# Compression dealt out into the projections, and prompt scores taken in pairs, in a two-layer decoder step

## The chip, the cores and the metric

The kernel runs on one core of one Trainium2 chip. The metric is the device time of one execution in microseconds. The engines are PE (TensorE matmuls), PEld (TensorE weight loads), DVE (VectorE), ACT (ScalarE), POOL (GpSimd) and SP (SyncE, which issues every DMA here).

## The reference

One inference step of a two-layer decoder for a prompt of 512 tokens and 8 x 8 sampled tokens (576 columns together). Layer 0 mixes with a convolution and stick-breaking attention, layer 1 with native sparse attention; each layer then has cross-attention into a memory and a SwiGLU FFN. The change lies in layer 1's mixer:

```python
def compress_blocks(kv, pe, w1, w2):
    ...
    blk = kv.reshape(B, nb, CMP_BLK, G, d) + pe[None, None, :, None, :]
    hid = jax.nn.gelu(jnp.einsum('bnlgd,ldh->bngh', blk, w1))
    return jnp.einsum('bngh,he->bnge', hid, w2)

def odd_mixer(...):
    u = a @ w_in
    ...
    kc = compress_blocks(ck_all, pe_k, w1_k, w2_k)
    vc = compress_blocks(cv_all, pe_v, w1_v, w2_v)
    ...
    o_cmp = jnp.einsum('bgrtn,bngd->btgrd', p_cmp.astype(vc.dtype), vc)
    o_sel = selected_branch(q, to_blocks(sk_all), to_blocks(sv_all), sel_idx, q_pos)
    o_win = window_branch(q, wk_all, wv_all, q_pos, w_pos)
    o = gates[..., 0:1] * o_cmp + gates[..., 1:2] * o_sel + gates[..., 2:3] * o_win
```

For the prompt the selected and the window branch are both a causal softmax attention over all 512 keys, so each needs scores, a softmax, a scaling by the gate and a product with the values.

## The kernel before

Every large product is `dense` (line 283): blocks of 256 output columns; in a block four PSUM groups (columns 0 to 255 and 256 to 575, for each 128 outputs), each group eight k-steps of three matmuls (L304, L305, L306: high and low halves in fp32r). The weights of the next block are loaded into a ring of three `raw` buffers and split (`wblock`, L262 to L272) while the block runs. `tick`, where given, is called after every second k-step and after each group, 16 times in a block.

The source order is a priority, not the order of issue: a planner that runs when the kernel is built places the instructions of each engine, earlier source first among those that its own model holds ready, and each engine then runs that list strictly in order. The trace shows such placing: the page loads of L1134 for the first three row tiles start at 540 us, 500 us ahead of the code around them, and transposes of one step stand between the matmuls of the next.

`odd_mixer` (layer 1) first projects the compressed branch's keys and values (`dense` into `ckv`, 512 columns), then the queries in four blocks `dq(0)` to `dq(3)` of 256 columns, each followed by `rope`. Around them `compress("k")` and `compress("v")` run, each in two halves of 16 positions (`h16`):

- rows: four tiles `kn` from the ring `KN` (three buffers), each of four page loads of 64 KB on SP (L1134), a DVE copy that reorders it (L1135), four PE transposes (L1139), four copies into `bt` (L139, L141); then nine small DVE copies of the prompt's own rows (L1150, L1151). `bt` is one buffer, `xtp`.
- hidden: four loads of first-layer weights `w1`, 512 KB each, into the `raw` ring (L1155), and 32 fp32 matmuls a half (L1161; each stands as two records in the trace, so 64 a half).
- after the second half the GELU and the load of `w2`, then the second-layer product.

The order in the source is: rows of k's first half, `dq(0)`, hidden of it, rows of the second half, `rows_out` (transposes and writes of `ckv`), `dq(1)`, hidden of it, k's second layer, then the same for v around `dq(2)` and `dq(3)`, v's second layer, and the projections of the other keys and values (`blk`).

The prompt's attention is `main`: 32 units (two head groups, four query blocks `j` of width 128 to 512 keys, two pairs of heads, two branches). In a unit `scores` makes four score tiles `z` in the PSUM ring `ACC` (four buffers): two fp32r matmuls (L1539 with the high, L1540 with the low half of the keys) and a bf16 matmul that adds the causal mask (L1541). Then come a maximum on DVE (L1542) and an exponential with its sum on ACT (L1543). After the fourth tile one reciprocal and one product with the gate make the factors `f` (L1546, L1548), and POOL multiplies the four tiles (L1552). The step `values` of an earlier unit, dealt between the tiles, transposes its four tiles key block by key block (L1563) and multiplies with the values (L1573); its first key block needs all four multiplied tiles. The steps are dealt as s s v0 s v1 s v2 v3 ..., where s is one tile's scores.

Of the kernel before, what the change touches and what calls it, by code (L numbers as in the profile page):

```python
# [94 lines left out]
def hybrid_step(ctx: ExitStack, tc: tile.TileContext, off, a, o):  # L95
# [984 lines left out]
    def odd_mixer(l):  # L1080
# [28 lines left out]
        def ev_to(dst, scale=None):  # L1109
            return lambda m, s0, n, p: ev_r(dst[:, m, s0:s0 + n], p, s0, scale)  # L1110
# [11 lines left out]
        dense(w, A, 0, 8, c0, 512, ev_to(ckv), nxt=(w, 0, 8, 0, 256, load_q, paired))  # L1122

        def compress(x):
            W = 161
            hps = [WK("hid0"), WK("hid1")]
            for h16 in range(2):
                bt = xtp.tile([128, 16 * W], FT, tag="bt", name="bt").rearrange("p (c n) -> p c n", n=W)
                for q4 in range(4):
                    kn = KN("cn")  # L1130
                    for i in range(4):
                        src = a["cache_nsa_cmp_" + x][0, ds(pages[q4 * 4 + i], 1)] \
                            .rearrange("a (n c l) g d -> (a n) c (l g d)", n=2, l=2)
                        nc.sync.dma_start(kn[i * 32:i * 32 + 32, 0:512], src[:, h16 * 16:h16 * 16 + 16])  # L1134
                    nc.vector.tensor_copy(kn[:, 512:1024].rearrange("p (g l d) -> p g l d", g=4, l=2),  # L1135
                                          kn[:, 0:512].rearrange("p (l g d) -> p g l d", l=2, g=4))
                    p = WK()
                    for g in range(4):
                        nc.tensor.transpose(p[:, g * 128:g * 128 + 128], kn[:, 512 + g * 128:640 + g * 128], ident)  # L1139
                    pv = p.rearrange("p (g b c) -> p g b c", g=4, c=16)  # L1140
                    for g in range(4):
                        evac(bt[:, :, q4 * 32:q4 * 32 + 32].rearrange("p c (b g) -> p g b c", g=4)[:, g], pv[:, g])
                cb = h16 * 16
                for g in range(4):
                    gp, gg = g // 2, g % 2
                    srow = ckv[gg * 64:gg * 64 + 64, (0 if x == "k" else 2) + gp, 0:TP] \
                        .rearrange("p (n c l) -> p c n l", n=8, l=2)
                    for l2 in range(2):
                        d_ = bt[l2 * 64:l2 * 64 + 64, :, 128:160].rearrange("p c (n g) -> p c n g", g=4)
                        nc.vector.tensor_copy(d_[:, :, :, g], srow[:, cb:cb + 16, :, l2])  # L1150
                nc.vector.tensor_copy(bt[:, :, 160], vt[:, vo["cmp_pe_" + x] + cb:vo["cmp_pe_" + x] + cb + 16])  # L1151
                yield
                for c4 in range(4):
                    w1 = wp.tile([128, 4, 256], FT, tag="raw", name="w1", bufs=3)
                    nc.sync.dma_start(w1, a["cmp_w1_" + x][0].rearrange("l d h -> (l d) h")  # L1155
                                      [(cb + c4 * 4) * 128:(cb + c4 * 4) * 128 + 512]
                                      .rearrange("(c p) h -> p c h", p=128))
                    for c in range(4):
                        cc = c4 * 4 + c
                        for m in range(2):  # L1160
                            nc.tensor.matmul(hps[m][:, :W], w1[:, c, m * 128:m * 128 + 128], bt[:, cc, :],  # L1161
                                             start=cb + cc == 0, stop=cb + cc == 31)
                if h16 == 0:
                    yield
            hid = ar[:, 0:320].rearrange("p (m n) -> p m n", m=2)
            hb = SML(2, "hb")
            for m in range(2):
                nc.vector.tensor_copy(hb[:, m:m + 1], hps[m][:, 160:161])
                nc.scalar.activation(hid[:, m, :], hps[m][:, 0:160], AF.Gelu_apprx_tanh, bias=hb[:, m:m + 1])
# [3 lines left out]
            yield  # L1173

        Vn = ar[:64, 4096:4608].rearrange("p (r f) -> p r f", r=2)
        cres = {}
        ck_, cv_ = compress("k"), compress("v")

        def dq(i):
            dense(w, A, 0, 8, i * 256, 256, ev_to(qT[:, i * 2:i * 2 + 2], 0.125), load_q, paired,  # L1180
                  nxt=(w, 0, 8, i * 256 + 256, 256, load_q, paired) if i < 3 else blk[0])
            rope(qT[:, i * 2:i * 2 + 2])
# [22 lines left out]

        next(ck_)
        dq(0)
        next(ck_)
        next(ck_)
        pump([rows_out(ckv, ("cmp_k", "cmp_v"))], 9)  # L1210
        dq(1)
        next(ck_)
        hid, w2 = cres["k"]
        p = WK()
        for m in range(2):
            nc.tensor.matmul(p[:64, 0:160], w2[:, m, :], hid[:, m, :], start=m == 0, stop=m == 1)
        kc, ksw, kr = ar[:64, 448:608], ar[:64, 608:768], ar[:64, 768:1088]
        kcs = cp.tile([128, 128], FT, name="kcs")
        nc.sync.dma_start(kr, a["c_ropec"])
        nc.vector.tensor_copy(kc, p[:64, 0:160])  # L1220
        nc.scalar.activation(ksw[0:32], p[32:64, 0:160], AF.Copy)
        nc.scalar.activation(ksw[32:64], p[0:32, 0:160], AF.Copy)
        nc.vector.tensor_mul(kc, kc, kr[:, 0:160])
        nc.vector.tensor_mul(ksw, ksw, kr[:, 160:320])
        for hh in range(2):
            nc.vector.tensor_add(kcs[hh * 64:hh * 64 + 64], kc[:, 0:128], ksw[:, 0:128])
        next(cv_)
        dq(2)
        next(cv_)
        next(cv_)  # L1230
        dq(3)
        next(cv_)
        hid, w2 = cres["v"]
        hx = ar[:, 1088:1344]
        hxv = hx.rearrange("p (m g r x n) -> p m g r x n", m=2, g=2, r=4, x=2)
        for m in range(2):
            for gp in range(2):
                for r in range(4):
                    nc.vector.tensor_copy(hxv[:, m, gp, r], hid[:, m, 128:160]
                                          .rearrange("p (n g x) -> p g x n", g=2, x=2)[:, gp])  # L1240
        p = WK()
        for m in range(2):
            nc.tensor.matmul(p[:, 0:64], hid[:, m, 0:128], w2[:, m, :], start=m == 0, stop=m == 1)
        evac(vcs, p[:, 0:64])
        p = WK()
        for m in range(2):
            nc.tensor.matmul(p[:, 0:64], hx[:, m * 128:m * 128 + 128], w2[:, m, :], start=m == 0, stop=m == 1)
        l2 = xtp.tile([128, 2560], FT, tag="bt", name="l2")
        vcz, pcT = l2[:, 0:1024], l2[:, 1024:1536]
        kcd = l2[:, 2048:2144]  # L1250
        nc.vector.memset(kcd, 0.0)
        kcv = kcd.rearrange("p (g x) -> p g x", g=2)
        for hh in range(2):
            nc.vector.tensor_add(kcv[hh * 64:hh * 64 + 64, :, 16 + hh * 8:24 + hh * 8],
                                 kc[:, 128:160].rearrange("p (n g x) -> p x g n", g=2, x=2)[:, hh],
                                 ksw[:, 128:160].rearrange("p (n g x) -> p x g n", g=2, x=2)[:, hh])
        nc.vector.tensor_tensor(vcz.rearrange("p (h d) -> p h d", d=64),
                                p[:, None, 0:64].to_broadcast([128, 16, 64]),
                                C("hsel", 16)[:, :, None].to_broadcast([128, 16, 64]), op=OP.mult)
# [11 lines left out]
        def cmp_prompt():  # L1271
            zt = WK("cmz")
# [222 lines left out]
        dense(w, A, 0, 8, blk[0][3], 256, ev_to(kk_[:, 0:2]), nxt=blk[1])  # L1495
# [36 lines left out]
        def scores(P, gp, j, rp, br):  # L1532
            n = (j + 1) * 128
            nm, sm, f = SML(4, "nm"), SML(4, "sm"), SML(4, "f")
            for x in range(4):
                gg = x // 2
                q = qd[gp, j, rp, gg][:, x % 2]
                z = ACC()
                nc.tensor.matmul(z[:, :n], q, kd[gp][:, gg, br, :n], start=True, stop=False)  # L1539
                nc.tensor.matmul(z[:, :n], q, kl[gp][:, gg, br, :n], start=False, stop=False)  # L1540
                nc.tensor.matmul(z[:, n - 128:n], identb, causb, start=False, stop=True)  # L1541
                last[0] = nc.vector.tensor_reduce(nm[:, x:x + 1], z[:, :n], axis=AX.X, op=OP.max, negate=True)  # L1542
                last[1] = nc.scalar.activation(P[:, x, :n], z[:, :n], AF.Exp, bias=nm[:, x:x + 1],  # L1543
                                               accum_out=sm[:, x:x + 1])
                if x == 3:
                    nc.vector.reciprocal(f, sm)  # L1546
                    f4 = f.rearrange("p (g r) -> p g r", g=2)
# [212 lines left out]
```

## Time and profile before

| what | us |
|---|---|
| runs: median (lowest to highest, 3 runs) | 2161.29 (2157.91 to 2163.09) |
| the profiled execution's own time | 2158.69 |
| its span from the first to the last instruction | 2156.8 |
| PE busy in the span | 2058.1 (95%) |
| TensorE's mean granted clock | 0.982 |

Times in rows are microseconds from the span's start unless marked ns. A matmul's recorded length includes the time in which it overlaps the next one, so the pace of PE is read from the distances between starts. The granted clock is a share of 2.4 GHz; 0.50 is the lower level, 1.2 GHz. The DMA share is a mean over the core's 16 DMA engines.

### The profile page before, as it was taken

The numbers are of one execution on the slowest core, as the hardware profiler recorded it, in microseconds if no ns is written. First come the engines' busy times: TensorE is split into PE (matmuls) and PEld (weight loads), VectorE is DVE, ScalarE is ACT, GpSimd is POOL, SyncE is SP. The second block draws the span as 40 slices with busy tenths as digits, with TensorE's granted clock in tenths as the row PEclk, the third lists the DMA queues.
The fourth block names the chain that finished last, engine by engine and source line by source line (L and its number), as shares of the span: only waits on it lengthen the run. The fifth ranks groups of instructions, "written<-read, shape, count | busy, mean of one in ns | idle before, by whom it ended". The sixth has DMA issues, their size and how long they took to land. (4 is left out here: it accounts for less than half of the span.)

```text
span 2156.8 us, 38247 instructions
## 1 busy us (share of the span) xinstructions
PE 2058.1 (95%) x15545; PEld 1901.2 (88%) x15545; DVE 1045.1 (48%) x1820; ACT 833.3 (39%) x1737; POOL 805.2 (37%) x752
## 2 busy tenths in 40 slices
PE   8999989999999999999878989999999999999998
PEld 7999846977999999999878967667887999999998
DVE  5479886445432332325344667654644432233333
ACT  6354554334332122224233546654443422132231
POOL 4365573412344142334212435553511344142342
PEclk9999998999999999999999989999999999999999
DMA  7454142256222222223344122311355222223232
GB/s 238 149 171 158 39 152 84 87 164 205 84 79 79 79 80 88 88 67 108 100 140 122 55 74 72 89 30 41 127 168 174 70 85 82 79 64 103 79 111 114
DMA packets 219358, 225.17 MB, mean 104 GB/s; under 512 B 13527, under 2 KB 208152, under 8 KB 219110
## 3 DMA queue, kind: packets, MB, share of 16 engines
q1 hardware_dynamic: 219181, 222.73, 33.3%
q8 instruction: 122, 2.00, 0.4%
q14 instruction: 55, 0.44, 0.1%
HBM read 210.04 MB, written 17.08 MB: 105 GB/s over the span
## 5 line engine op out<-in xcount | busy, mean ns | idle before, releaser
L304 PE MATMUL acc<-aH,wh 128*128 128x320 f32 (+1 forms) x2320 | 698.1, 301 | 0.0
L306 PE MATMUL acc<-aH,wl 128*128 128x320 f32 (+1 forms) x2320 | 692.2, 298 | 0.0
L305 PE MATMUL acc<-aL,wh 128*128 128x320 f32 (+1 forms) x2320 | 691.4, 298 | 0.0
L304 PEld LDWEIGHTS acc<-aH,wh 128*128 128x128 f32 x2320 | 442.5, 191 | 5.8 <-issue 4.5
L306 PEld LDWEIGHTS acc<-aH,wl 128*128 128x128 f32 x2320 | 442.3, 191 | 4.3 <-issue 4.1
L305 PEld LDWEIGHTS acc<-aL,wh 128*128 128x128 f32 x2320 | 442.3, 191 | 2.8 <-issue 2.5
L268 ACT ACTIVATE wh<-raw 128x1024 fp32r<-128x1024 f32 (+2 forms) x270 | 260.8, 987 | 433.8 <-PE acc L305 158.8
L272 POOL TENSOR_TENSOR wl<-raw,wh 128x1024 fp32r<-128x1024 f32 (+2 forms) x100 | 229.0, 2293 | 386.2 <-ACT wh L268 356.8
L270 DVE TENSOR_TENSOR wl<-raw,wh 128x1024 fp32r<-128x1024 f32 (+3 forms) x170 | 242.7, 1437 | 92.1 <-ACT wh L268 90.3
L305 PE MATMUL acc<-fL,wh 128*128 128x320 f32 (+1 forms) x592 | 175.6, 297 | 0.0
L304 PE MATMUL acc<-fH,wh 128*128 128x320 f32 (+1 forms) x592 | 175.6, 297 | 0.0
L306 PE MATMUL acc<-fH,wl 128*128 128x320 f32 (+1 forms) x592 | 175.5, 297 | 0.0
L337 DVE TENSOR_TENSOR h<-acc,h 128x320 f32<-128x320 f32 (+1 forms) x176 | 79.7, 455 | 195.6 <-PE acc L306 178.8
L998 POOL TENSOR_TENSOR sg<-sg,rs 128x256 f32<-128x256 f32 (+1 forms) x88 | 87.7, 999 | 154.2 <-ACT sg L997 153.5
L1005 POOL TENSOR_TENSOR fL<-sg,fH 128x256 fp32r<-128x256 f32 (+1 forms) x88 | 89.0, 1011 | 132.8 <-ACT fH L1004 132.0
L221 POOL TENSOR_TENSOR ssq<-ssq,tmp 128x256 f32<-128x256 f32 (+1 forms) x84 | 81.0, 968 | 146.2 <-ACT tmp L220 145.7
L1552 POOL TENSOR_TENSOR nar<-nar,f 128x512 f32<-128x512 f32 (+3 forms) x128 | 92.4, 752 | 106.6 <-DVE f L1548 93.1
L1003 DVE TENSOR_TENSOR sg<-acc,sg 128x256 f32<-128x256 f32 (+1 forms) x88 | 40.1, 456 | 166.3 <-PE acc L306 156.7
L242 DVE TENSOR_TENSOR sg<-acc,rs 128x256 f32<-128x256 f32 (+1 forms) x88 | 39.8, 456 | 159.2 <-PE acc L306 156.5
L306 PEld LDWEIGHTS acc<-fH,wl 128*128 128x128 f32 x592 | 112.5, 190 | 0.0
L304 PEld LDWEIGHTS acc<-fH,wh 128*128 128x128 f32 x592 | 112.5, 190 | 0.0
L305 PEld LDWEIGHTS acc<-fL,wh 128*128 128x128 f32 x592 | 112.5, 190 | 0.0
(433 smaller groups left out, 3958.7 us busy)
## 6 DMA issues: line engine op xcount, KB each, us to landing
raw<-in_w_ffn_gate_dram SPq DMA_DIRECT2D x40, 512.0 KB
raw<-in_w_ffn_up_dram SPq DMA_DIRECT2D x40, 512.0 KB
ck<-in_cache_mem_k_dram SPq DMA_DIRECT2D x32, 512.0 KB
cv<-in_cache_mem_v_dram SPq DMA_DIRECT2D x32, 512.0 KB
raw<-in_w_ffn_down_dram SPq DMA_DIRECT2D x32, 512.0 KB
raw<-in_w_in_even_dram SPq DMA_DIRECT2D x20, 512.0 KB
raw<-in_w_mem_k_dram SPq DMA_DIRECT2D x16, 512.0 KB
raw<-in_w_mem_v_dram SPq DMA_DIRECT2D x16, 512.0 KB
```

Source lines behind the costliest of these rows:

```text
L221: nc.gpsimd.tensor_add(acc, acc, t)
L268: last[1] = nc.scalar.activation(hi, x, AF.Copy)
L270: nc.vector.tensor_sub(lo, x, hi)
L272: nc.gpsimd.tensor_sub(lo, x, hi)
L304: nc.tensor.matmul(po, WH[:, k, ms], H[:, k, s], start=k == 0, stop=False)
L305: nc.tensor.matmul(po, WH[:, k, ms], L[:, k, s], start=False, stop=False)
L306: nc.tensor.matmul(po, WL[:, k, ms], H[:, k, s], start=False, stop=k == nk - 1)
L337: nc.vector.tensor_add(h[:, m, s0:s0 + n], p, h[:, m, s0:s0 + n])
L998: nc.gpsimd.tensor_mul(t, t, rs[s0])
L1003: nc.vector.tensor_mul(t, p, t)
L1005: nc.gpsimd.tensor_sub(HL[:, b0 + m, s0:s0 + n], t, HH[:, b0 + m, s0:s0 + n])
L1552: nc.gpsimd.tensor_tensor(Py, Py, f[:, y:y + 1].to_broadcast([128, n]), op=OP.mult)
```

## The change

1. The compression is cut into generators that `dense` calls at its ticks: `cmp_rows` (rows; one step loads and reorders a tile, the next transposes it), `cmp_hidden` (hidden; two matmuls a tick), `finish_k`, `finish_v`. Rows of k's first half run in the `ckv` projection, hidden of one half and rows of the next run together in one `dq`, `rows_out` and hidden of v's second half in `dq(3)`, `finish_v` in the first `blk` projection.
2. `bt` has two places, by halves: `xtp` and the start of `S2`, which is free until the `blk` projections write there.
3. `w1` leaves the `raw` ring for the two buffers of `KT`, loaded one ahead.
4. `scores` takes its four tiles in two pairs: both masks first, then the four fp32r matmuls, two maxima, two exponentials; then, as a step of its own, the pair's reciprocal, its product with the gate and its two multiplications on POOL. The number of steps of a unit (four) and the dealing order stay.

The work computed is the same, except that there are 64 reciprocals and 64 gate products of two columns where there were 32 of each of four.

```diff
-        def compress(x):
...
+        def cmp_rows(x, h16):
+            if h16:
+                bt = S2[:, 0:16 * W].rearrange("p (c n) -> p c n", n=W)
+            else:
                 bt = xtp.tile([128, 16 * W], FT, tag="bt", name="bt").rearrange("p (c n) -> p c n", n=W)
...
+                nc.vector.tensor_copy(kn[:, 512:1024].rearrange("p (g l d) -> p g l d", g=4, l=2),
+                                      kn[:, 0:512].rearrange("p (l g d) -> p g l d", l=2, g=4))
+                yield 1
...
+                yield 1
...
+        def w1_load():
+            while w1_todo and len(w1s) < 2:
+                x, c = w1_todo.pop(0)
+                w1 = KT("w1").rearrange("p (c h) -> p c h", c=4)
...
+        def cmp_hidden(x, h16):
...
+                for c in range(4):
+                    cc = c4 * 4 + c
+                    for m in range(2):
+                        nc.tensor.matmul(hps[x][m][:, :W], w1[:, c, m * 128:m * 128 + 128], bt[:, cc, :],
+                                         start=cb + cc == 0, stop=cb + cc == 31)
+                    if c == 3:
+                        w1_load()
+                    yield 1
...
+        dense(w, A, 0, 8, c0, 512, ev_to(ckv), nxt=(w, 0, 8, 0, 256, load_q, paired), tick=run((rows["k", 0], 4, 3)))
+        pump(rows["k", 0], 99)
+        cmp_new("k", 0)
+        w1_load()
...
+        dq(0, ([cmp_hidden("k", 0)], 1, 1), (rows["k", 1], 0, 2))
+        cmp_new("k", 1)
+        dq(1, ([cmp_hidden("k", 1)], 1, 1), (rows["v", 0], 0, 2))
+        cmp_new("v", 0)
+        dq(2, ([cmp_hidden("v", 0)], 1, 1), (rows["v", 1], 0, 2), ([finish_k()], 2, 3))
+        cmp_new("v", 1)
+        dq(3, ([cmp_hidden("v", 1)], 1, 1), ([rows_out(ckv, ("cmp_k", "cmp_v"))], 0, 3))
...
+        dense(w, A, 0, 8, blk[0][3], 256, ev_to(kk_[:, 0:2]), nxt=blk[1], tick=run((fv, 2, 4)))
...
-            for x in range(4):
...
-                    for y in range(4):
-                        Py = P[:, y, :n]
-                        nc.gpsimd.tensor_tensor(Py, Py, f[:, y:y + 1].to_broadcast([128, n]), op=OP.mult)
-                yield 1
+            for gg in range(2):
+                zs = [ACC() for r in range(2)]
+                for z in zs:
+                    nc.tensor.matmul(z[:, n - 128:n], identb, causb, start=True, stop=False, skip_group_check=True)
+                for r, z in enumerate(zs):
+                    q = qd[gp, j, rp, gg][:, r]
+                    nc.tensor.matmul(z[:, :n], q, kd[gp][:, gg, br, :n], start=False, stop=False, skip_group_check=True)
+                    nc.tensor.matmul(z[:, :n], q, kl[gp][:, gg, br, :n], start=False, stop=True, skip_group_check=True)
...
+                yield 1
+                fx = f[:, gg * 2:gg * 2 + 2]
+                nc.vector.reciprocal(fx, sm[:, gg * 2:gg * 2 + 2])
+                nc.vector.tensor_mul(fx, fx, gkv[:, j, gp, rp * 2:rp * 2 + 2, gg, 1 + br])
+                for x in (gg * 2, gg * 2 + 1):
+                    nc.gpsimd.tensor_tensor(P[:, x, :n], P[:, x, :n], f[:, x:x + 1].to_broadcast([128, n]),
+                                            op=OP.mult)
                 yield 1
```

In a `run` job the two numbers are the first tick and the distance in ticks at which the generator advances one step.

## Rows read from the trace of the kernel before

**Rows 1.** The page's head and part 1: span; engine busy us (share) xinstructions

```profile
span 2156.8 us, 38247 instructions
...
PE 2058.1 (95%) x15545; PEld 1901.2 (88%) x15545; DVE 1045.1 (48%) x1820; ACT 833.3 (39%) x1737; POOL 805.2 (37%) x752
```

**Rows 2.** Stretches: us, busy us (xinstructions) by engine, granted clock, DMA share, GB/s

```profile
1022.00:1052.00 30.00, 30.00 (x234) 30.00 (x234) 14.59 (x32) 7.14 (x16) 7.64 (x7) 1.00 0.26 74
...
1052.00:1186.00 134.00, 110.54 (x755) 107.11 (x754) 62.35 (x157) 44.91 (x80) 22.08 (x20) 0.92 0.44 131
...
1246.00:1300.00 54.00, 47.67 (x299) 31.24 (x300) 38.72 (x72) 26.52 (x66) 21.59 (x21) 0.84 0.23 66
...
1300.00:1400.00 100.00, 95.74 (x790) 68.81 (x786) 67.82 (x175) 68.43 (x201) 51.46 (x72) 1.00 0.29 81
...
1400.00:1500.00 100.00, 91.13 (x652) 69.98 (x652) 54.77 (x128) 49.17 (x145) 49.44 (x68) 0.98 0.09 27
```

**Rows 3.** Waits of PE in 1052 to 1186: waiter <- releaser: us, times, longest

```profile
PE wk L1139 <- DVE cn L1135: 10.4, 4, 4.6
...
PE hid L1161 <- DMA w<-in_cmp_w_k_dram: 5.5, 2, 3.9
```

**Rows 4.** DMA view of 1058 to 1071: queue, packets, MB, share; then issues

```profile
q1 hardware_dynamic: 374, 0.66, 13.2%
...
cn<-in_cache_nsa_cmp_k_dram SPq DMA_DIRECT2D x7, 64.0 KB
```

**Rows 5.** Two more stretches, columns as in rows 2

```profile
1086.00:1088.00 2.00, 2.00 (x19) 2.00 (x18) 0.81 (x3) 0.41 (x1) 0.00 (x0) 1.00 1.00 291
...
1107.00:1111.00 4.00, 1.45 (x11) 1.21 (x9) 2.66 (x5) 0.81 (x1) 1.32 (x2) 1.00 0.35 118
```

**Rows 6.** Timeline of SyncE's issues and of PE: start, us, line, xcount [idle <-releaser]

```profile
540.80 10.79 SPq L1134 DMA_DIRECT2D cn<-in_cache_nsa_cmp_k_dram  x12
...
1048.32 3.15 SPq L1134 DMA_DIRECT2D cn<-in_cache_nsa_cmp_k_dram  x4
...
1098.88 5.74 SPq L1134 DMA_DIRECT2D cn<-in_cache_nsa_cmp_v_dram  x7
...
1104.73 0.40 SPq L1155 DMA_DIRECT2D w<-in_cmp_w_k_dram  x1
...
1112.38 1.98 PE L1161 MATMUL hid<-bt,w 128*128 128x161 f32 x6 [3.93 <-DMA w<-in_cmp_w_k_dram]
```

**Rows 7.** Waits of PE in 1240 to 1505, columns as in rows 3

```profile
PE ntp L1563 <- POOL nar L1552: 13.7, 29, 1.5
```

**Rows 8.** Groups by shape, 1240 to 1505: xcount | busy, mean ns | idle

```profile
L1552 POOL TENSOR_TENSOR nar<-nar,f 128x512 f32<-128x512 f32 x32 | 35.5, 1139 | 36.5 <-DVE f L1548 30.5 <-PE wk L1424 5.8
...
L1546 DVE RECIPROCAL f<-sm 128x4 f32<-128x4 f32 x32 | 5.6, 175 | 9.6 <-ACT nar L1543 9.2
```

**Rows 9.** Timeline of POOL and PE around the scores, columns as in rows 6

```profile
1254.94 5.01 POOL L1552 TENSOR_TENSOR nar<-nar,f 128x512 f32<-128x512 f32 x4 [6.90 <-DVE f L1548]
...
1385.12 0.48 PE L1539 MATMUL acc<-kd,qd 128*128 128x512 f32 x1
...
1385.43 0.40 PE L1540 MATMUL acc<-kl,qd 128*128 128x512 f32 x1
...
1385.67 0.23 PE L1541 MATMUL acc<-causb,identb 128*128 128x128 bf16 x1
...
1385.71 0.48 PE L1539 MATMUL acc<-kd,qd 128*128 128x512 f32 x1
```

**Rows 10.** Timeline of PE in the compression, columns as in rows 6

```profile
1069.30 6.74 PE L1161 MATMUL hid<-bt,w 128*128 128x161 f32 x48
...
1080.67 0.36 PE L304 MATMUL acc<-aH,wh 128*128 128x256 f32 x1
...
1080.87 0.28 PE L305 MATMUL acc<-aL,wh 128*128 128x256 f32 x1
...
1080.99 0.28 PE L306 MATMUL acc<-aH,wl 128*128 128x256 f32 x1
```

More of the change, by code (lines that the diff above doesn't have):

```diff
@@ new lines, in cmp_new @@
+        def cmp_new(x, h16):
+            bt, cb = bts[x, h16], h16 * 16
+            for g in range(4):
+                gp, gg = g // 2, g % 2
+                srow = ckv[gg * 64:gg * 64 + 64, (0 if x == "k" else 2) + gp, 0:TP] \
+                    .rearrange("p (n c l) -> p c n l", n=8, l=2)
+                for l2 in range(2):
+                    d_ = bt[l2 * 64:l2 * 64 + 64, :, 128:160].rearrange("p c (n g) -> p c n g", g=4)
+                    nc.vector.tensor_copy(d_[:, :, :, g], srow[:, cb:cb + 16, :, l2])
+            nc.vector.tensor_copy(bt[:, :, 160], vt[:, vo["cmp_pe_" + x] + cb:vo["cmp_pe_" + x] + cb + 16])
@@ L1172, in compress, with run, f, dq @@
             cres[x] = hid, w2
-            yield
+        def run(*jobs):
+            n = [0]
+            def f():
+                for gens, first, every in jobs:
+                    if n[0] >= first and (n[0] - first) % every == 0:
+                        pump(gens, 1)
+                n[0] += 1
+            return f
+        rows = {k: [cmp_rows(*k)] for k in (("k", 0), ("k", 1), ("v", 0), ("v", 1))}
+        dense(w, A, 0, 8, c0, 512, ev_to(ckv), nxt=(w, 0, 8, 0, 256, load_q, paired), tick=run((rows["k", 0], 4, 3)))
+        pump(rows["k", 0], 99)
+        cmp_new("k", 0)
+        w1_load()
         Vn = ar[:64, 4096:4608].rearrange("p (r f) -> p r f", r=2)
-        cres = {}
-        ck_, cv_ = compress("k"), compress("v")
-        def dq(i):
+        def dq(i, *jobs):
             dense(w, A, 0, 8, i * 256, 256, ev_to(qT[:, i * 2:i * 2 + 2], 0.125), load_q, paired,
-                  nxt=(w, 0, 8, i * 256 + 256, 256, load_q, paired) if i < 3 else blk[0])
+                  nxt=(w, 0, 8, i * 256 + 256, 256, load_q, paired) if i < 3 else blk[0], tick=run(*jobs))
+            for gens, _, _ in jobs:
+                pump(gens, 99)
             rope(qT[:, i * 2:i * 2 + 2])
@@ L1204, in rows_out @@
                 yield 1
[L1206 to L1216, printed above, removed]
         kc, ksw, kr = ar[:64, 448:608], ar[:64, 608:768], ar[:64, 768:1088]
         kcs = cp.tile([128, 128], FT, name="kcs")
-        nc.sync.dma_start(kr, a["c_ropec"])
@@ L1220, in odd_mixer @@
[L1220 to L1256, printed above, removed]
@@ L1271, in cmp_prompt @@
         def cmp_prompt():
+            l2 = l2_[0]
+            pcT, kcd = l2[:, 1024:1536], l2[:, 2048:2144]
             zt = WK("cmz")
@@ L1534, in scores @@
             nm, sm, f = SML(4, "nm"), SML(4, "sm"), SML(4, "f")
-            for x in range(4):
[L1536 to L1547, printed above, removed]
-                    nc.vector.tensor_mul(f4, f4, gkv[:, j, gp, rp * 2:rp * 2 + 2, :, 1 + br]
-                                         .rearrange("p r g -> p g r"))
-                    for y in range(4):
-                        Py = P[:, y, :n]
-                        nc.gpsimd.tensor_tensor(Py, Py, f[:, y:y + 1].to_broadcast([128, n]), op=OP.mult)
```

131 lines of the change are left out of this document (84 added, 47 removed).

## The prediction

> **What bounds the kernel now.** I read the page's busy shares first: PE is busy for 2058 of 2157 us, no other engine for half of that [rows 1]. So only what keeps PE idle, or slow, can be won. Then the view of stretches, over the part that the diff touches. In the `ckv` projection PE is busy throughout at a granted clock of 1.00. From there to the end of the compression, 1052 to 1186, it is busy for 110.5 of 134 us at a clock of 0.92: 23.5 us idle, and (1 - 0.92) x 110.5 = 8.8 us of busy time lost to stretches at the lower level, 1.2 GHz; together 32.3 us. In the prompt's attention the three stretches from 1246 to 1500 show 6.3, 4.3 and 8.9 us idle, and clocks of 0.84, 1.00 and 0.98, so 7.6 + 1.9 = 9.5 us lost; together 29.0 us [rows 2]. These 61 us are all that the two halves of the change can recover.
>
> The view of waits names the causes. In the compression PE waits 10.4 us for the reordering copy of a row tile and 5.5 us for k's first-layer weights [rows 3]; in the attention 13.7 us for POOL's multiplications [rows 7]. The DMA view says why rows and weights are late. From 1058 to 1071 page loads run alone, seven of them issued inside that stretch: 0.66 MB in 13 us is 51 GB/s, and the share of 13.2% of 16 engines is 2.1 engines [rows 4]. A load of all engines moves 291 GB/s at a share of 1.00 [rows 5]. So queued page loads do not spread: each occupies one pair of engines for 64 KB / 50 GB/s = 1.3 us, a row tile 5.2 us. The weights that share this pair queue behind: a `w1` issued at 1104.73, after seven page loads, is used at 1112.38, 7.65 us later [rows 6], while PE is busy for 1.45 of 4 us and the DMA engines are 35% busy [rows 5].
>
> The Trainium skill (DMA: Bandwidth & Descriptors, Why a DMA increments its semaphore by 16 and not by 1) says that a copy runs on the largest number of engines up to 16 that divides the slowest dimension of both sides, and on the lowest-numbered ones; a page's slice has a slowest dimension of 2. By that all page loads here share one and the same pair, which the rows suggest but do not show, and no order of the source can spread them; if they did spread, the 11 us of lateness below would be zero and the sum 40.5 instead of 29.5 us.
>
> **The change, compression.** The edits and their costs:
>
> *Filling.* Hidden and transposes go between the dense matmuls, in time to be waited for much later than they are loaded. The three first row tiles are loaded at 540 us already [rows 6] and should be again. With k's first half transposed at ticks 7, 13, 19 and 25 of the `ckv` projection's 32 (some 0.9 us each, from 1022 on), their buffers come free from about 1028 on, not 1048, so the pair of DMA engines starts some 20 us earlier. If nothing else were late, all 32.3 us would come back.
>
> *What the pair of engines still holds.* A tick in `dq` is two dense k-steps and four hidden records. Dense: 96 matmuls at 30.0/234 = 0.128 us [rows 2] = 12.3 us a block; hidden: 64 records at 6.74/48 = 0.14 us [rows 10] = 9.0; 16 transposes at about the same 0.13 = 2.1; switches (below) 1.3; together 24.7 us a block, 6.2 us for a quarter of it. In that quarter the pair has to move one row tile (5.2), its part of one `w1` (512 KB at 291 GB/s, 1.8) and of the next projection weights (256 KB, 0.9): 7.9 us. Where the next rows are loaded at full pace, in `dq(0)` and `dq(1)`, eight quarters, PE can be late by 8 x 1.7 = 13.6 us; `dq(2)` and `dq(3)` have slack. The head start from the `ckv` projection takes a part of it: nothing if the queue is full when `dq(0)` begins, all of it at best. The buffers of k's first half come free one by one up to some 7 us before that, each followed by a load of 5.2, so the queue begins nearly empty; a `w1` behind an empty queue lands within its quarter, and the lead of 6.2 - 1.8 us less its issue and landing, some 2 us, covers the first one or two quarters. The other six and a half cost 1.7 each: 11 us, all of it waits on `w1`; bounds 0 and 13.6.
>
> *Own buffers for `w1`.* With two buffers a load is issued when its predecessor's predecessor is done and needed a quarter (6.2 us) later. In the trace the bad case took 7.65 us; SP adds up to 7 page issues x 0.82 = 5.7 us ahead of it [rows 6], though usually four. That lateness is the 11 us above, not a second one. The projection weights no longer share the ring with `w1`; nothing in the rows charges PE for that, so zero.
>
> *Switches.* After fp32 transposes the first dense matmul starts 0.20 us before the second, against 0.12 for the next [rows 10]: 0.08 us to enter. 64 hidden ticks make 64 entries, 5.1 us, of which blocks of hidden paid perhaps 1 before: 4 us more.
>
> *The clock.* If the 11 us gather in a few stalls of 3 to 4 us, like the longest ones before (3.9 and 4.6 [rows 3]), the lower level follows some of them. I keep 2 us of the 8.8 as lost.
>
> *Moved work.* `rows_out` goes from between `dq(0)` and `dq(1)` to `dq(3)`, with its ten writes on SP; there no page loads are queued, so zero. `finish_k` and `finish_v` go into blocks with PE work beside them; v's two products waited 1 to 2 us before. DVE, busy for 62 of 134 us, and ACT, for 45, get nothing new; if a copy that waits for a page blocked DVE for 3 us, the four `ACC` buffers cover three groups, about 9 us. A `bt` in `S2` and the 64 x 2 small copies cost nothing then.
>
> Sum: 32.3 - 11 - 4 - 2 = 15 us won; from 5 (each of 14 reloads later by 0.7 us than in the walk) to 28.
>
> **The change, scores.** *POOL.* Before, four multiplications follow the fourth exponential: 4 x 1.139 = 4.6 us at 512 keys [rows 8], and the first block in the trace waited 6.9 us for its factors, then took 5.0 [rows 9]. Now two tiles are multiplied while the other two are scored, and the second pair is scored one dealing step earlier. The last tile is ready 2 x 1.139 = 2.3 us sooner at 512 keys. All 29 waits on POOL sum to 13.7 us, none longer than 1.5 [rows 7]; a shift of that size ends most. What is late next is DVE and ACT: the second pair's maxima and exponentials. I take 10, bounds 0 (another wait ends last) and 13.7.
>
> *Order on PE.* A tile starts every 0.59 us: 0.31 from the high to the low half, 0.24 to the mask, 0.04 on [rows 9]. The 0.31 against 0.24 is the entry after the mask; in pairs it is paid once for two tiles: 64 x 0.07 = 4.5, less the second mask of a pair, not covered by a long matmul, about 0.02 each: 3 us, bounds 0 and 4.5.
>
> *Costs.* 32 more reciprocals (0.175 us [rows 8]) and as many gate products of about the same cost put 11 us on DVE, busy for 161 of 254 us [rows 2], and each reciprocal now stands on DVE behind the pair's two exponentials, with evacuations behind it. A pair takes two of four `ACC` buffers at once. I take 3 us on the path, bounds 0 and 8.
>
> *The clock.* The longest slow stretch follows the first unit's waits on POOL. If these go, the clock stays up: half of 9.5, 4.5 us; bounds 0 and 9.5.
>
> The first block's multiplications took 5.01/4 = 1.25 us each, the mean is 1.14 [rows 8, 9]. The Trainium skill (SBUF — State Buffer, SBUF: two separate sides) says that a GpSimd instruction and a VectorE one with two SBUF inputs lock one port pair in turn for a whole instruction, which speaks against multiplying beside more DVE work. If all 32 x 2 multiplications that now start earlier at 512 and 384 keys lost 0.11 us so, that would be 7 us on POOL, and the sum 22.5 instead of 29.5; the rows cannot tell this cause from others.
>
> Sum: 10 + 3 - 3 + 4.5 = 14.5 us won; from 0 to 26.
>
> Both: 29.5 us. PE stands at 95% over the whole span [rows 1], and neither half touches what follows these stages, so a gain is kept to the end. The profiled execution took 2158.7, 2.6 under the median of 2161.3; from the median, 2131.8, from the profiled one 2129.2. I say 2131.
>
> **The rivals.** (1) *The pair of engines decides.* Page loads, not order, set the compression's end: the same bytes, the same pair. It then recovers only the start's part, 5 us, and the scores 12: 2144. For it: constant 51 GB/s; against it: 20 us of earlier start. (2) *The planner does not follow.* The lists are placed by its model; it can bunch hidden again or put the pair's second half where the old fourth tile was. Half of both gains: 2146. (3) *Slower: late weights at every reload.* Two buffers, a quarter of 6.2 us, and queue plus landing of 7.65 + 3.3 (four page issues) make each of 14 reloads late by 4.7 us, 66 us, with the clock down at each, 8 more; less 32 recovered and 14.5 from the scores: 27 longer, 2188. It decides from a mean lateness of (32 + 14.5 - 4)/14 = 3 us. For it: one measured 7.65; against it: that one stood behind seven page loads.
>
> **How the numbers follow.** Forecast 0.63, (1) 0.13, (2) 0.11, (3) 0.13. The forecast's own range is 2107 (gains of 28 and 26) to 2148 (13 in all); (1) and (2) lie a few us to either side of their times. The range is 2107 to 2152; out of it are (3) and the tails. What a measurement can tell from no change is about 0.2%, 4 us. Faster: 0.62 of the forecast, 0.11 of (1), 0.09 of (2), 0.82; the same: 0.06, the rest of these three and of (3); slower: 0.12, from (3).
>
> **What would show it.** Right: in the stretch of the compression PE idle falls from 23.5 to about 11 us, with the waits on `w1` (`KT`) ahead of those on rows, and page loads still at 50 GB/s; hidden stands in groups of four records between dense matmuls; the wait of transposes on POOL falls under 5 us and the clock from 1246 to 1300 rises over 0.9. Wrong: waits on `w1` over 40 us, hidden in runs of 48 as now, or waits of the score tiles on ACT in place of those on POOL.

## The result, and the profile after

The kernel after takes 2128.6 us (median of 4 runs, 2128.2 to 2129.0), the one before 2162.2 beside it: a ratio of 0.9846 (95% interval 0.9828 to 0.9864), 33.6 us less. The forecast was 2131.0, in a range of 2107 to 2152. The time was hit; what stands behind it was hit only in part, because terms that were too low and too high offset each other.

The profiled execution of after took 2129.0 us. Its page's head and part 1, for [rows 1]:

```profile
span 2127.2 us, 38324 instructions
...
PE 2045.2 (96%) x15545; PEld 1902.4 (89%) x15545; DVE 1058.4 (50%) x1884; ACT 834.0 (39%) x1737; POOL 803.1 (38%) x752
```

Three marks of the timeline part the two halves of the change: the first dense matmul of the `ckv` projection, the write of the sampled tokens' gates on SP, after the projections (L1500 before, L1544 after), and the first activation of the next norm, after the attention. In after they stand here (start, us, engine, line):

```profile
1021.87 0.28 PE L304 MATMUL acc<-aH,wh 128*128 128x256 f32 x1
...
1206.13 0.34 SPq L1544 DMA_DIRECT2D gd<-nar  x1
...
1476.76 0.51 ACT L213 ACTIVATE aH<-h,vt 128x256 fp32r<-128x256 f32 x1 [1.52 <-DVE h L337]
```

Before they stand at 1019.90, 1215.15 and 1507.21. So the *compression* (first to second mark) went from 195.25 to 184.26 us, 11.0 less, and the *attention* (second to third) from 292.06 to 270.63, 21.4 less. Together 32.4; the spans differ by 29.6 because after reaches the first mark 2.0 us later and loses 0.8 behind the third. The 2.0 are no effect of the change: in the runs below the first mark lies between 1017.8 and 1022.8, over code that is the same. The lengths between marks repeat better than whole times: kernels with the same code for a stage agree within 1.4 us in the compression and within 2.1 in the attention (table below), and the reading goes by them.

The stretches of after, columns as in [rows 2]; the first two end the compression, the last three are the attention but for its first 31 us:

```profile
1052.00:1158.00 106.00, 91.93 (x633) 89.84 (x631) 52.36 (x114) 38.04 (x69) 19.39 (x17) 0.92 0.43 132
1158.00:1206.13 48.13, 45.76 (x334) 43.76 (x334) 29.73 (x60) 25.78 (x38) 15.64 (x14) 1.00 0.23 71
...
1237.00:1290.00 53.00, 45.31 (x312) 30.60 (x310) 41.53 (x84) 27.98 (x72) 23.62 (x24) 0.94 0.23 67
1290.00:1390.00 100.00, 95.39 (x820) 72.43 (x816) 78.12 (x212) 68.87 (x203) 57.21 (x76) 1.00 0.30 88
1390.00:1476.76 86.76, 86.12 (x658) 70.54 (x657) 52.80 (x149) 47.80 (x140) 43.04 (x64) 1.00 0.16 40
```

Cut into PE's idle time, time lost to the lower clock level ((1 - clock) x busy) and the rest, which is busy time at full clock, each by the same marks:

| stage | idle before, after | lost clock before, after | rest before, after |
|---|---|---|---|
| compression | 24.9, 16.4 | 8.8, 7.4 | 161.5, 160.5 |
| attention | 19.5, 13.0 | 9.6, 2.7 | 262.9, 254.9 |

The compression won 8.5 us of idle time and hardly any clock. The attention won 6.5 us of idle time, 6.9 of clock, and 8.0 in which PE was booked as busy. The split is rough. The clock has two places only; summed over slices of 2 us, after's lost clock is 7.3 us in the compression and 3.3 in the attention (9.5 before). Kernels of the table below that share a stage's code differ too: 4.5 to 7.3 us of lost clock in after's compression (four kernels), in the attention 6.6 to 9.5 with the scores of before (three) and 3.1 to 4.6 with those of after (eight). The rest moves little: in those attentions it is 263.0 to 264.1 us and 254.2 to 254.7.

What PE waited for in after, in the compression (1022 to 1206) and then in the attention (from 1206); columns as in [rows 3] and [rows 7]:

```profile
PE hid L1180 <- DVE hb L1190: 3.9, 1, 3.9
PE hid L1180 <- DMA w<-in_cmp_w_k_dram: 3.7, 2, 3.2
PE hid L1180 <- DVE kvA L141: 3.3, 1, 3.3
PE hid L1180 <- issue: 2.2, 1, 2.2
PE hid L1180 <- DMA w<-in_cmp_w_v_dram: 1.7, 1, 1.7
...
PE ntp L1609 <- POOL nar L1597: 4.8, 6, 1.6
PE wk L1414 <- DVE csz L1410: 2.5, 1, 2.5
```

The copies of rows no longer head the list, and POOL's part fell from 13.7 us to 4.8, as forecast. But weights make only 5.4 us of the compression's waits; 9.4 stand on DVE and on "issue", which the prediction put at nothing. The timeline shows what these are (DVE and PE around 1116, then DVE and ACT ahead of the wait of 3.3 us, which ended at 1088.59):

```profile
1116.59 0.43 DVE L1137 COPY cn<-cn 128x512 f32<-128x512 f32 x1 [3.34 <-DMA cn<-in_cache_nsa_cmp_v_dram]
...
1118.01 0.19 DVE L1190 COPY hb<-hid 128x1 f32<-128x1 f32 x2
...
1118.27 1.42 PE L1180 MATMUL hid<-bt,w 128*128 128x161 f32 x4 [3.90 <-DVE hb L1190]
```

```profile
1080.36 0.43 DVE L1137 COPY cn<-cn 128x512 f32<-128x512 f32 x1 [3.69 <-DMA cn<-in_cache_nsa_cmp_v_dram]
...
1080.93 0.48 DVE L244 SCALAR_TENSOR_TENSOR nq<-acc,rs 128x320 f32<-128x320 f32 x1
...
1081.44 2.80 ACT L1102 ACTIVATE nar<-nq 32x576 f32<-32x576 f32 x4 [4.34 <-DVE nq L244]
```

DVE stands for 3.34 us at the reordering copy of a row tile, which waits for its page. Behind it, in DVE's fixed order, stands the small copy `hb` that frees the PSUM tiles that v's hidden writes; PE waits 3.90 us for that. So the late page is the cause here too, by way of DVE's queue. The 2.2 us at 1055 came in the same way: DVE waited 2.87 us at a copy for its page until 1053.29, then a `bt` copy, then PE. The 3.3 us came by one step more. DVE stood for 3.69 us at a copy for its page until 1080.36; behind it stood the evacuation of a dense group whose last matmul had started at 1076.36. `rope` on ACT and DVE needs that evacuation, and the copies of rows into hidden's input stood behind `rope`. So in the trace all 9.4 us lead back to DVE standing at a copy for its page.

### The profile page after: what moved, and what is told of

Same layout as the page of the kernel before. It is cut to its first block, busy times and chain, and to the rows that moved or that the text cites. A ratio compares the mean times of both kernels' runs of the same rounds, so it can differ in the third digit from the quotient of the medians.

```text
span 2127.2 us, 38324 instructions
## 1 busy us (share of the span) xinstructions
PE 2045.2 (96%) x15545; PEld 1902.4 (89%) x15545; DVE 1058.4 (50%) x1884; ACT 834.0 (39%) x1737; POOL 803.1 (38%) x752
```

## The experiments

Compression and attention are measured between the marks above, in one profiled execution each; times are medians, ratios those to the kernel before on the same chip.

| kernel | us | ratio (95% interval) | compression | attention |
|---|---|---|---|---|
| before | 2162.2 | 1 | 195.25 | 292.06 |
| after | 2128.6 | 0.9846 (0.9828 to 0.9864) | 184.26 | 270.63 |
| compression alone | 2150.1 | 0.9939 (0.9924 to 0.9955) | 184.25 | 291.57 |
| scores alone | 2139.5 | 0.9897 (0.9880 to 0.9913) | 193.87 | 270.11 |
| after, pages spread | 2107.1 | 0.9739 (0.9724 to 0.9753) | 165.38 | 271.86 |
| before, pages spread | 2134.0 | 0.9864 (0.9845 to 0.9883) | 168.75 | 292.54 |
| after, pairs multiplied late | 2142.8 | 0.9914 (0.9895 to 0.9933) | 185.26 | 285.07 |
| after, single tiles multiplied early | 2128.1 | 0.9844 (0.9823 to 0.9864) | 183.99 | 268.77 |
| after, row copy on POOL | 2125.2 | 0.9833 (0.9815 to 0.9851) | 182.42 | 271.39 |
| after, `w1` in the `raw` ring | 2123.0 | 0.9829 (0.9810 to 0.9848) | 181.44 | 271.32 |
| pages spread, again | 2108.3 | 0.9762 (0.9737 to 0.9787) | 165.16 | 271.26 |
| pages spread, `w1` in the `raw` ring | 2105.4 | 0.9748 (0.9726 to 0.9770) | 163.46 | 270.14 |
| pages spread, hidden in bunches of eight | 2105.8 | 0.9746 (0.9724 to 0.9768) | 162.60 | 272.18 |
| pages spread, single tiles multiplied early | 2101.7 | 0.9729 (0.9707 to 0.9752) | 165.30 | 266.84 |

### Each half alone

The edit puts the `scores` of the one kernel into the other; nothing else changes.

> The new compression with the scores of before (tiles one by one, four multiplications at the end). Theory of the traces: between the start of the ckv projection and the gate's write the trace of after is 11.0 us shorter (195.25 to 184.26), and nothing of that comes from the scores, so 2162 - 11 = 2151. By the prediction's sum this half wins 15: 2147. Rival: the two halves need each other (the earlier end of the compression lets the first unit start with its keys ready), then each alone wins less than its part: over 2155.

> The paired scores with the compression of before. Theory of the traces: from the gate's write to the next stage after is 21.4 us shorter (292.06 to 270.63), so 2162 - 21.4 = 2141, with POOL's wait of PE near 5 us and the clock of the first stretch near 0.94. By the prediction's sum 14.5: 2148. Rival: halves depend on each other: under 10 us won, over 2152.

Ratios of 0.9939 and 0.9897 are 13.2 us (9.7 to 16.4) and 22.3 us (18.8 to 26.0) of 2162.8. Their sum, 35.5, is the 33.6 of both within the intervals, and each stage's length is that of after in the kernel that has the new half and about that of before in the other. The halves do not need each other. The lengths read from the traces of after, 2151 and 2141 for the halves, were the better forecast; the prediction's sums, 2147 and 2148, were not.

### Do the page loads share one pair of DMA engines?

```diff
-                        .rearrange("a (n c l) g d -> (a n) c (l g d)", n=2, l=2)
-                    nc.sync.dma_start(kn[i * 32:i * 32 + 32, 0:512], src[:, h16 * 16:h16 * 16 + 16])
+                        .rearrange("a (n c l) g d -> c (a n) (l g d)", n=2, l=2)
+                    nc.sync.dma_start(kn[i * 32:i * 32 + 32, 0:512], src[h16 * 16:h16 * 16 + 16])
...
-                pv = p.rearrange("p (g b c) -> p g b c", g=4, c=16)
+                pv = p.rearrange("p (g b c n) -> p g b c n", g=4, c=16, n=2)
```

The copies into `bt` follow the same order. The bytes, the pieces of 2 KB and the number of loads stay.

> The kernel after, with each page load read in the order (16 positions, 2 blocks) instead of (2, 16): same bytes, same number of loads, slowest dimension 16; the copies behind the transposes put the columns back. If a page load sits on one pair of engines because its slowest dimension is 2, it now goes over 16: page loads run at over 200 GB/s while they are alone, a tile takes about 1 us instead of 5.2, and the waits that stand behind late pages go: 2.2 + 3.7 + 3.9 + 1.7 = 11.5 us idle and about 4 to 5 of the 7.4 us of clock, so 2128.6 - 16 = 2113 (2108 to 2119). Rival (the rate of 50 GB/s is that of a queue of small pieces of 2 KB, whatever the engines): no change in rate and time, 2126 to 2130. Rival (the fixed order of DVE and SP holds the stalls): loads fast, time above 2123.

> The kernel before with the same reading order of page loads. If the one pair of engines made most of the loss of before, the waits on the reordering copy (10.4 us) and on weights (8.0) go with part of 8.8 us of clock: 15 to 22 us won, about 2143, and dealing out would be worth little beside it. If the order (rows and hidden in blocks with no dense work between) made it, then PE still waits in row blocks for the chain copy, transposes, copies: under 8 us won, 2155 or more.

The DMA view of 1047 to 1053, first of after, then of after with pages spread (40 slices of 0.15 us: tenths of the 16 engines' time, and GB/s; then the issues, with the time to landing at the end):

```profile
DMA  9551122212111111111111111111111111111111
GB/s 273 150 99 44 58 96 99 96 68 75 65 41 55 55 55 55 41 55 41 55 55 55 55 41 55 55 41 55 55 55 41 55 55 41 55 55 55 55 41 55
...
cn<-in_cache_nsa_cmp_k_dram SPq DMA_DIRECT2D x6, 64.0 KB
```

```profile
DMA  0059100283004640015400000000000000000000
GB/s 14 14 137 259 41 27 0 68 259 110 0 0 82 205 150 0 0 55 219 164 0 0 0 0 0 0 0 0 0 0 0 0 0 0 0 0 0 0 0 0
...
cn<-in_cache_nsa_cmp_k_dram SPq DMA_DIRECT2D x3, 64.0 KB, 2.2
```

In after a queue of page loads runs at an even 41 to 55 GB/s without end. Spread, each load is a burst of up to 259 GB/s, landed 2.2 us after its issue, and between two bursts there is nothing: now SP's issuing, not the transfer, sets the pace. So the pair was real, and the time follows: 21.5 us between the two medians, 18.9 of them in the compression; at 2107.1 it lies just under the 2108 to 2119 expected. The stretch and the largest wait of after with pages spread:

```profile
1052.00:1158.00 106.00, 102.21 (x770) 100.86 (x769) 61.22 (x143) 45.72 (x80) 23.96 (x21) 1.00 0.48 141
...
PE hid L1180 <- DMA w<-in_cmp_w_v_dram: 1.7, 1, 1.7
```

Idle time between the marks falls from 16.4 to 5.5 us, and the clock is 1.00 throughout: 10.9 + 7.4 us. In the old order the same edit does still more, 26.5 us of the compression; its waits on the copy (10.4 us, [rows 3]) and on weights shrink to these, and the largest that stays is 2.6 us for a copy into `bt`:

```profile
PE wk L1139 <- DVE bt L141: 2.6, 1, 2.6
PE wk L1139 <- DVE cn L1135: 1.1, 1, 1.1
...
PE hid L1161 <- DMA w<-in_cmp_w_k_dram: 0.2, 1, 0.2
PE hid L1161 <- DMA w<-in_cmp_w_v_dram: 0.2, 1, 0.2
```

So dealing out is worth 11.0 us where pages are slow and 3.4 (168.75 less 165.38) where they are not: it covered part of a loss that could be taken away at its source. (The 3.4 are one trace against another, where the stage repeats within 1.4.) The Trainium skill (DMA: Bandwidth & Descriptors, Why a DMA increments its semaphore by 16 and not by 1) lets a copy run on the largest number of engines up to 16 that divides the slowest dimension of both sides; from 2 to 16 in that dimension is what this edit changes, and the bursts agree.

### Who holds the hidden matmuls up: DVE's queue or the pages?

```diff
-                nc.vector.tensor_copy(kn[:, 512:1024].rearrange("p (g l d) -> p g l d", g=4, l=2),
+                nc.gpsimd.tensor_copy(kn[:, 512:1024].rearrange("p (g l d) -> p g l d", g=4, l=2),
```

> The kernel after with the reordering copy of a row tile on POOL instead of DVE. A copy that waits for its page then no longer holds up DVE's later work. If the stalls of 2.2 us (before hidden of k) and 3.9 us (hidden of v on the copy of hb) come from DVE's queue standing behind a copy that waits for a page, they go, with the half-clock time behind them: 6 to 9 us won, 2120 to 2122. If the pages themselves set the end (a transpose needs the copy anyway), the waits move to the transposes: within 2 us, 2127 to 2130. If POOL's splits for dense are now held up instead: slower, over 2131.

```profile
PE hid L1180 <- DMA w<-in_cmp_w_k_dram: 10.1, 4, 5.9
PE hid L1180 <- DMA w<-in_cmp_w_v_dram: 5.3, 2, 3.6
```

The waits on DVE and on issue, 9.4 us in after, are gone, and the waits on weights went from 5.4 to 15.4 us. The compression is only 1.8 us shorter, its idle time 16.8 us for 16.5, the time 2125.2 for 2128.6 with intervals that overlap. That lies between the two cases expected, 6 to 9 us and nothing. DVE's queue was the way that the lateness took, not its size: whatever first needs something that the pair delivers late is charged with the wait.

### Own buffers for the weights

```diff
-                w1 = KT("w1").rearrange("p (c h) -> p c h", c=4)
+                w1 = wp.tile([128, 4, 256], FT, tag="raw", name="w1", bufs=3)
```

> The kernel after with w1 back in the raw ring of three buffers that it shares with the projection weights, all else dealt out as in after. The prediction put the own buffers at zero beside the lateness of the pair of engines: 2128.6, within 3. Rival (own buffers matter: in the ring a w1 waits for the split of the projection weights before it, and the projection weights for hidden): each of 14 loads later by 1 us or more, and the clock down behind them: over 2145.

> Spread page loads and w1 back in the raw ring of three. On the kernel after this moved the compression from 184.3 to 181.4 us. If that was the third buffer giving late weights more room, it is worth nothing once pages no longer hold the weights up: compression within 1 us of 165.4, 2106 to 2108. If own buffers matter (projection weights held up by w1): compression over 168, 2110 or more. If sharing is better by itself: under 163.5.

With slow pages the compression is 2.8 us shorter without own buffers, with spread pages 1.7 (163.46 against 165.16), little over the 1.4 us within which the stage repeats. The whole times point the same way, their intervals overlap. The own buffers are no part of the gain; a small loss is likely and not shown beyond doubt. With slow pages the time, 2123.0, missed the 2128.6 "within 3" that was expected. Why sharing should be better is not tested.

### What a switch between hidden and dense costs

```diff
-                    yield 1
+                    if c % 2:
+                        yield 1
...
-        dq(0, ([cmp_hidden("k", 0)], 1, 1), (rows["k", 1], 0, 2))
+        dq(0, ([cmp_hidden("k", 0)], 1, 2), (rows["k", 1], 0, 2))
```

The other three `dq` likewise.

> The kernel after with spread page loads (as in the third experiment), once more, as the base of the three beside it on the same chip: 2107, compression 165.4 us from the first matmul of the ckv projection to the gate's write.

> Spread page loads and hidden in bunches of eight records at every second tick, so 32 switches from hidden to dense in place of 64. By the prediction's price of 0.08 us a switch: 2.6 us won, compression 162.8. By the cycle read in after (six dense matmuls and four hidden records in 1.25 us, their sum apart 0.72 + 0.56 = 1.28) a switch costs nothing: within 0.7 us of 165.4.

The compression went from 165.16 to 162.60, the 2.6 us that the price of 0.08 gives. But the idle time in it shows another way to that number: the waits listed for PE sum to 4.7 us in the base and to 2.2 with bunches (v's weights' wait of 1.7 is gone). That leaves 0.1 us for 32 switches. The time in which PE is busy between the marks, where a switch would be booked, agrees: 159.9 us in the base and 159.7 with bunches, both at a clock of 1.00. So does the timeline of after (one cycle of PE):

```profile
1061.06 0.71 PE L1180 MATMUL hid<-bt,w 128*128 128x161 f32 x4
1061.50 0.39 PE L304 MATMUL acc<-aH,wh 128*128 128x256 f32 x1
1061.72 0.28 PE L305 MATMUL acc<-aL,wh 128*128 128x256 f32 x1
...
1062.31 0.71 PE L1180 MATMUL hid<-bt,w 128*128 128x161 f32 x4
```

The first dense matmul does stand 0.22 us before the second, 0.10 over the pace of [rows 10]. But the four hidden records ahead of it take 0.44 from their start to its start, not 4 x 0.14 = 0.56. The cycle is 1.25 us, and six dense at 0.12 and four hidden at 0.14 make 1.28.

### Order on PE or early multiplication?

Of the two edits of `scores` each kernel keeps one: pairs with everything multiplied after the second pair, or single tiles with the mask last, of which every second is followed by

```diff
+                if x % 2:
+                    fx = f[:, gg * 2:gg * 2 + 2]
+                    nc.vector.reciprocal(fx, sm[:, gg * 2:gg * 2 + 2])
...
+                    for y in (gg * 2, gg * 2 + 1):
```

> The kernel after, but the pairs keep only their order on PE; one reciprocal, one gate product and all four multiplications stand after the second pair, as before. What is lost against after is the early multiplication alone. By the prediction's terms that is 10 (waits on POOL) + 4.5 (clock) less about 1.5 of the 3 us of costs: 2128.6 + 13 = 2142. If by the traces the order on PE won 7.9 and the rest 13.5 (6.6 idle, 6.9 clock): 2142 as well, with PE's wait for POOL back over 10 us. Rival: the multiplications' start matters little because the values come two units later: under 5 us lost, 2133.

> The kernel after, but tiles are scored one by one with the mask last, as before; each two tiles are multiplied as soon as the second is scored. What is lost is the order on PE (and the second step of a pair is one tile, not none). Prediction's term: 3 (0 to 4.5): 2131.6. By the traces 7.9 us less busy time of PE with the idle time and the clock set apart: 2136.5. Rival: nothing lost, 2128.6, where the busy time fell only because there are fewer restarts after waits.

> Spread page loads, tiles scored one by one with the mask last, each two multiplied as soon as they are scored. On the kernel after this left the time as it was (attention 268.8 us against 270.6). If pairing on PE is worth nothing beside early multiplication: attention 269 to 272, 2105 to 2109. If that was chance and pairing is worth the 4.5 us of its pace: attention over 274, 2111.

Waits of PE on POOL in the attention, first pairs multiplied late, then single tiles multiplied early:

```profile
PE ntp L1611 <- POOL nar L1599: 13.1, 23, 1.3
```

```profile
PE ntp L1606 <- POOL nar L1594: 4.1, 6, 2.2
```

Pairs without the early multiplication keep 13.1 us of waits on POOL and win 7.0 us of 21.4. Single tiles with it win 23.3, all and a little more. So the early multiplication is the gain, and the order on PE, worth 7 us alone, adds nothing to the length beside it. Of those 7 us, 6.4 are clock and 2.3 busy time at full clock (summed over slices of 2 us), less 1.7 of added idle time. The clock differs by up to 2.9 us between kernels with the same scores, so how much of the 6.4 the order makes is open. With spread pages single tiles are even 4.4 us shorter than pairs (266.84 against 271.26), which puts this kernel at 2101.7, the fastest measured: 59 us under before, though 2101.7 and the base's 2108.3 have overlapping intervals. What differs is 3.2 us of idle time and 2.8 of clock, mostly in the 55 us or so in which the first units run; busy time at full clock is even 1.5 us shorter with pairs. 2.5 of the idle time are one wait, that at L1414 in the list of after above (a transpose of the compressed branch). It stands at 2.5 us in all eight kernels with after's scores, and in neither with single tiles multiplied early. In after DVE shows where it comes from:

```profile
1256.07 0.17 DVE L1594 RECIPROCAL f<-sm 128x2 f32<-128x2 f32 x1 [3.19 <-ACT nar L1590]
...
1258.00 1.21 DVE L1410 TENSOR_TENSOR csz<-csz,rc 64x1024 f32<-64x1024 f32 x1
```

DVE stood for 3.19 us at a pair's reciprocal, which waits for the pair's exponentials, and the work of the compressed branch stood behind it. Single tiles have the same 64 reciprocals and not this wait, so it is the place of the reciprocal in DVE's list; why the planner puts it there with pairs is not shown.

## Why the prediction was right, and where it was not

**What bounds, and how much can be won:** right. 32.3 us were named as recoverable in the compression; dealing out and spread pages together won 29.9 us. But "these 61 us are all" was too narrow: it counts idle time and clock only, and 8 of the 21.4 us that the attention won came out of PE's busy time. Of the signs on record page loads at 50 GB/s, hidden in fours, waits on POOL under 5 us (4.8) and a clock over 0.9 (0.94) came; idle time of about 11 us in the compression did not, it is 16.4.

**The pair of DMA engines:** right, and it was put as a suggestion of the rows; the experiment shows it. The sentence on what would be if pages did spread (40.5 us in all, 2121) won too little: the run gave 2107, mainly since that sum kept 4 us of switches and 2 of clock and had 14.5 for the scores.

**Lateness, 11 us:** right in size (spread pages take 10.9 us of idle time away), wrong in form, so the size is in part luck. It was to be "all of it waits on `w1`"; 5.4 us were, and 9.4 came by way of DVE. The step that failed is "if a copy that waits for a page blocked DVE for 3 us, the four `ACC` buffers cover three groups": the block came, of 2.87, 3.69 and 3.34 us, but what stood behind it were copies for hidden itself, or `rope` ahead of such copies, which no `ACC` buffer covers. Beside it 5.5 us of idle time stay even with spread pages; the sum had nothing for these.

**The clock, 2 us kept as lost:** the worst-sized term; 7.4 us were lost in after, 4.5 to 7.3 in the four kernels with its compression. The stretches of 4 us behind three of the stalls show it (clock is the third column from the right):

```profile
1072.00:1076.00 4.00, 4.00 (x20) 3.96 (x19) 0.43 (x1) 0.18 (x1) 0.00 (x0) 0.57 0.40 142
...
1088.00:1092.00 4.00, 3.42 (x16) 3.38 (x17) 3.51 (x10) 3.88 (x7) 0.00 (x0) 0.65 0.31 89
...
1116.00:1120.00 4.00, 1.73 (x7) 1.76 (x8) 3.22 (x10) 2.58 (x5) 1.52 (x2) 0.57 0.30 106
```

The lateness did gather in a few stalls of 2.2 to 3.9 us, the prediction's own condition, and after each of them the lower level followed. Pricing the 11 us that it foresaw at the rate of [rows 2], 8.8 us of clock for 23.5 idle, would have kept 4 (an estimate).

**Switches, 4 us:** nothing that shows. The step read one interval, the entry to dense, and not the cycle: the hidden before it is shorter by as much.

**Own buffers and moved work at zero:** right as far as it goes; own buffers are nought or a loss of 2 to 3 us.

So the compression: 15 forecast, 11.0 in the traces (9.7 to 16.4 by its own run). In the prediction's own terms: idle time 8.5 won where 23.5 - 11 = 12.5 were forecast, clock 1.4 for 6.8, and busy time at full clock 1.0 won where 4 were to be lost in switches. One term set too low offset two set too high.

**Scores, waits on POOL (10) less costs (3):** right. The waits on POOL fell by 8.9 us, all idle time by 6.5. The added work on DVE is there (64 reciprocals of 160 ns for 32 of 175), and the cost was the one that the prediction names, a reciprocal on DVE behind the pair's exponentials with other work behind it: the 2.5 us at L1414. POOL's multiplications at 512 keys did not get longer, for the 1139 ns of [rows 8]:

```profile
L1597 POOL TENSOR_TENSOR nar<-nar,f 128x512 f32<-128x512 f32 x32 | 34.6, 1102 | 31.9 <-DVE f L1595 21.7 <-ACT nar L1590 4.1 <-PE ntp L1609 2.8
```

Those at 384 keys went from 826 to 876 ns, and all 128 together take 93.9 us where they took 92.3. The turn-taking at one port pair of which the Trainium skill tells (SBUF — State Buffer, SBUF: two separate sides) would have cost 7 us by the prediction's estimate; POOL's total rose by 1.6, and no run here tells the turns from other causes.

**Clock, 4.5 us:** 6.9 (6.2 in slices of 2 us); the stretch after the first unit rose from 0.84 to 0.94, and the last one to 1.00.

**Order on PE, 3 us (0 to 4.5):** near in size, 2.0 us of busy time by the order alone (262.9 to 260.9), but only 0.8 beside the early multiplication (255.7 to 254.9), less than the wait at L1414 takes. The term that was missing stands beside it: early multiplication by itself took 7.2 us of PE's busy time away (262.9 to 255.7). A likely reason is that a wait costs more than its idle time: a transpose's record averages 0.28 us, and four in a row take 0.60:

```profile
1364.28 0.60 PE L1609 MATMUL ntp<-ident,nar 128*128 128x128 f32 x4
...
1368.26 0.27 PE L1609 MATMUL ntp<-ident,nar 128*128 128x128 f32 x1
```

That is 0.11 each at pace and 0.17 of tail, which at a wait is booked as busy and not overlapped. By this estimate 23 waits fewer (29 to 6) make 3.9 us of the 7.2; no run tests it, and the rest is open.

So the scores: 14.5 forecast, 21.4 in the traces (18.8 to 26.0 by its own run). Too little won by clock and busy time here covers too much in the compression: 29.5 forecast, 32.4 between the marks.

**The rivals.** (1), the pair decides, was half true: the pair sets the loss in both kernels, but dealing out won 11 us all the same, not 5. (2), the planner does not follow: no, hidden stands in fours between dense. (3), late weights at every reload: no; 5.4 us of waits on 14 reloads, 15.4 even where DVE holds nothing up, against 42 from which it would have turned.

## What to carry to other kernels

Before work is dealt out to cover a slow transfer, see on how many DMA engines it runs: an even low rate in the DMA view, while the share stands at one or two tenths, was cured here by another dimension order in the access pattern, for 19 us where the dealing gave 11. A late resource shows up as a wait on whatever reaches it first, so a wait's name is no cause until a run has moved it. On an engine that runs a fixed list, look at what stands behind an instruction that waits: a copy for its page and a reciprocal for its exponentials each held up other work here. Try releasing a consumer early by halves (two tiles of four) before touching the order on PE, and price a wait at its idle time, the tail of the record before it and the clock behind it.

## What the hardware showed that was not expected

Page loads of the same bytes in the same pieces went from an even 41 to 55 GB/s to bursts of 259 when only the order of their dimensions changed, and DVE's copies into hidden's input behind them did not get longer (392 ns in after, 377 with pages spread). Stalls of 2.2 to 3.9 us in the compression were each followed by some 3 to 5 us at the lower clock level (0.57 to 0.69 over stretches of 4 us), while with spread pages, where no listed wait is over 1.7 us, the granted clock stayed at 1.00. The length of a stall alone does not decide: in the old order with spread pages PE stood for 2.6 us and the clock stayed at 1.00. And alternating fp32 hidden with fp32r dense matmuls in fours cost nothing that 64 switches would show.
